# The first chunk of h and of the merged branches begins at the weights' place in a row of 256 bytes

## The chip, the core and the metric

The kernel runs on one core of one Trainium2 chip. The metric is the device time of one execution in microseconds (us); lower is better. TensorE (PE) multiplies matrices: it loads a stationary operand of 128 x 128 numbers (a weight load, shown as PEld) and then streams a moving operand past it. VectorE (DVE) and ScalarE (ACT) do elementwise work, GpSimd (POOL) little here, SyncE (SP) issues the DMAs that bring weights from memory into SBUF, the core's working memory of 128 partitions.

Addresses matter in this change. Every operand begins at some byte of its partition; this text calls that address modulo 256 the operand's **place**.

## The reference

Two layers on 256 tokens of width 2048, all in float32:

```python
h = rmsnorm(x, norm_mix[l]) * (1.0 + sc_a) + sh_a
qa, ka, va, qb, kb, vb, ga, gb = split_cols(h @ w_in[l])
ya = window_attention(...) @ w_proj_a[l]            # 8 heads of 128
yb = neighbourhood_attention(...) @ w_proj_b[l]     # 8 heads of 128
merged = sigmoid(ga) * ya + sigmoid(gb) * yb
x = x + gt_a * (merged @ w_out[l])
h = rmsnorm(x, norm_ffn[l]) * (1.0 + sc_m) + sh_m
u = depthwise_conv(h @ w_up[l], conv_w[l], conv_b[l])
g, v = split(u)                                     # 2 x 5632
x = x + gt_m * ((silu(g) * v) @ w_down[l])
```

The six modulation vectors (`sc_a`, `sh_a`, ...) are a matrix-vector product of `silu(c)` with `ada_w`.

## The kernel before

**Two-part numbers.** Each float32 factor is held as a high part and a rest, both in the type float32r. A product is three matmuls: high times high, high times rest, rest times high. `unit` brings 16 weight blocks of 128 x 128 in one DMA of 1 MB, then splits each half of them into `hl`: ACT copies the high part (L240), DVE subtracts (L241). There are 232 such units in a layer and four `hl` buffers, reused in turn.

**Two kinds of product.** `features` makes 128 output features for all 256 tokens: `feature_block` (L245 to L251) loads the weights (`hl`) as the stationary operand and streams the activation chunk as the moving one, 256 columns; L249 is weight-high with activation-high, L250 weight-high with activation-rest, L251 weight-rest with activation-high. These three lines, in this order, are one *group*; a block of outputs is one group per 128 rows of the contraction, 16 for `h` and `merged`. `tokens` (L325 to L327) makes q, k and v: there `h` is stationary and four weight blocks, 512 columns, are the moving operand.

**Order of the work.** In a layer: q, k, v and the first gate (in layer 0 the contraction is cut into parts of 2, 4, 5 and 5 chunks, in layer 1 it is whole), with attention heads interleaved in the background; the projection of branch A (`oA`, 8 chunks); the second gate from `h`; the projection of branch B (`oB`), merged and split into `merged`; `w_out` on `merged`; then the FFN in three rounds, each of up-projections from `h` and down-projections from the activations `act`. The modulation's weights are streamed past DVE (L172) at a written pace beside all this. The program's order is that of the code; every engine runs its own queue in that order and waits on semaphores.

**Places.** `OFF, ROW = 48, 64` are counted in 4-byte words: 192 and 256 bytes. The pools are laid out one after the other, and `skip` puts small unused tiles between them. The four `hl` buffers begin at place 32; in units that hold q, k or v weights the data starts `OFF` words later, at 224. `skip(4 * OFF)` (L120) moves the pool of `h` to place 224; `merged` takes the same tile in its turn. All chunks are multiples of 1024 bytes, so each of the 16 chunks of `h` and `merged` begins at 224, and so do the buffers of the pool `ev` behind it (tag `u`: the last two `oA`, some gates, the convolution's scratch), those of `at` (`p`, `pT`, `qn`) and, after `skip(64)`, the pool `s` with `oA`, `oB`, `act` and the packed q, k, v. So a feature group has its moving operand at 224 and its weights at 32, save where a unit of layer 0 holds both q/k/v blocks and gate blocks: there both are at 224. In `tokens` both operands are at 224.

Of the kernel before, what the change touches and what calls it, by code (L numbers as in the profile page):

```python
# [9 lines left out]
F32 = mybir.dt.float32  # L10
F32R = mybir.dt.float32r
# [4 lines left out]
P = 128  # L16
L = 2
D = 2048
S = 256
KC = D // P  # L20
# [77 lines left out]
OFF, ROW = 48, 64  # L98
# [7 lines left out]
def encoder(ctx: ExitStack, tc: tile.TileContext, a: dict, out: bass.AP):  # L106
# [4 lines left out]
    def skip(n, p=None):  # L111

        skips.append((p or pool(f"skip{len(skips)}", 1)).tile([P, n // 4], F32, name=f"skip{len(skips)}"))
        nc.vector.memset(skips[-1][:], 0.0)
# [2 lines left out]
    lay = pool("lay", 2)  # L117
    rawp = pool("raw", 4)
    hlp = pool("hl", 4)
    skip(4 * OFF)  # L120
    hp = pool("h", 1)
    ev = pool("ev", 3)
    at = pool("at", 2)
# [22 lines left out]
        nc.scalar.activation(out=cact[:, i : i + 512], in_=cb[:], func=AF.Silu)  # L146
    x = const.tile([P, KC, S], F32, name="x")
    skip(96, const)
    skip(64)
    sp = pool("s", 1)  # L150

    def place(tag, n, dt, name):
        return sp.tile([P, n, S], dt, name=name, tag=tag)

    def chunks_of(p, tag, n, name):

        t = p.tile([P, n, 2, S], F32R, name=name, tag=tag)
        return [t[:, k] for k in range(n)]

    mods, amods, nrms, done = {}, {}, {}, {0: 0, 1: 0}  # L160

# [170 lines left out]
    def split(dst, src):  # L332
        nc.scalar.copy(dst[:, 0], src)
        nc.vector.tensor_tensor(out=dst[:, 1], in0=src, in1=dst[:, 0].bitcast(F32), op=ALU.subtract)

    def warm(n):

        if n:
            ps = ax.tile([P, 512], F32, name="warm", tag="ax")
            for _ in range(n):  # L340
                tc.keep_in_program_order(nc.tensor.matmul(ps[:, :P], ident[:], ident[:], start=True, stop=True))
# [32 lines left out]

    def normed(l, w, sums, st, first=False):

        h = chunks_of(hp, "h", KC, f"h{l}_{w}")

        def steps():
            ss = mean_sq  # L380
            if not first:
                ss = sm.tile([P, 2], F32, name="nss", tag="nss")
                ins = nc.vector.tensor_tensor(out=ss[:], in0=sums.head[:], in1=sums.ps[:, 1], op=ALU.add)
                st.hold(ins.ins, HELD)
            rs = sm.tile([P, 2], F32, name="nrs", tag="nrs")
            nc.gpsimd.tensor_tensor(out=rs[:], in0=ss[:], in1=mhalf[:, :2], op=ALU.pow)
            if not first:
                warm(WARM[1])
            rb = ax.tile([P, 512], F32, name="rb", tag="ax")
            for t in range(2):  # L390
                tc.keep_in_program_order(
                    nc.tensor.transpose(rb[:, t * P : (t + 1) * P], rs[:, t : t + 1].broadcast_to([P, P]), ident[:])
                )
            warm(WARM_IN if first else WARM[2])
            if first:
                rbs = ev.tile([P, S], F32, name="rbs", tag="sqa", bufs=1)
                nc.scalar.copy(rbs[:], rb[:, :S])
                rb = rbs
            mod, amod = mods[l], amods[l]
            for kc in range(KC):  # L400
                if not first:
                    need(l, 48 * w + 2 * kc + 2)
                t = ev.tile([P, S], F32, name="ht", tag="z")
                sh = mod[:, 3 * w * KC + kc : 3 * w * KC + kc + 1]
                nc.vector.scalar_tensor_tensor(
                    out=t[:], in0=x[:, kc], scalar=amod[:, w, kc : kc + 1], in1=rb[:, :S], op0=ALU.mult, op1=ALU.mult
                )
                nc.scalar.activation(out=h[kc][:, 0], in_=t[:], func=AF.Identity, bias=sh)
                nc.vector.scalar_tensor_tensor(  # L409
                    out=h[kc][:, 1], in0=t[:], scalar=sh, in1=h[kc][:, 0].bitcast(F32), op0=ALU.add, op1=ALU.subtract  # L410
                )
                yield

        return h, steps()
# [89 lines left out]
    def urgent(yes):  # L504
        return tc.high_priority() if yes else nullcontext()
# [21 lines left out]
    def need(l, n):  # L527

        while done[l] < n:
            next(adas)  # L530
# [54 lines left out]
    for l in range(L):  # L585
        st = Stream(l) if l == 0 else nxt
        h, steps = normed(l, 0, None if l == 0 else sums, st, first=l == 0)
# [17 lines left out]
        def va(k, g):  # L605
            return packs[0][:, 2 * k + 1, g * HEAD : (g + 1) * HEAD]

        ready, heads = [0], [0]
        oA, oB = [], []

        def head_a(i):
            g = i // (HA // GA)
            if i >= 6:
                oA.append(ev.tile([P, 2, S], F32R, name=f"oA{l}_{i}", tag="u", bufs=2))
            elif i % 2 == 0:
                o = place(("y0", "y1", "y2")[i // 2], 4, F32R, f"oA{l}_{i}")
                oA.extend((o[:, :2], o[:, 2:]))
            yield
            yield from attend(
                qTa[:, i], kTa[:, g], lambda k: va(k, g), tables[0], SCALE, sink[:, i : i + 1], lambda: oA[i],  # L620
            )
# [105 lines left out]
        gb = []  # L727
        for tag in ("y0", "y1", "y2"):
            t = place(tag, 4, F32, f"gb{l}_{tag}")
            gb += [t[:, i] for i in range(4)]  # L730
        for i in range(2):
            t = ev.tile([P, 2, S], F32, name=f"gb{l}_{i}", tag="u", bufs=2)
            gb += [t[:, 0], t[:, 1]]

        def gate_b(mo):
# [5 lines left out]
        for mo in range(KC):  # L741
            st.features(hs, [gate_b(mo)])
        bg.finish(job)
        merged = chunks_of(hp, "h", KC, f"merged{l}")
        for mo in range(KC):

            def merge(ps):
# [29 lines left out]


        h, steps = normed(l, 1, sums, st)
        with urgent(True):  # L780
            for _ in range(FEED):
# [4 lines left out]
        def conv(ps, ch, u):  # L786
            w = cw[:, ch]
            nc.scalar.activation(out=u, in_=ps, func=AF.Identity, scale=w[:, 1:2], bias=w[:, 3:4])  # L788
            for j, to, of in ((0, slice(1, S), slice(0, S - 1)), (2, slice(0, S - 1), slice(1, S))):
                nc.vector.scalar_tensor_tensor(  # L790
                    out=u[:, to], in0=ps[:, of], scalar=w[:, j : j + 1], in1=u[:, to], op0=ALU.mult, op1=ALU.add
                )

        for gi, chunks in enumerate(FF_GROUPS):
            acts = []
            for tag, n in (("b0", 12), ("b1", 12), ("y1", 4), ("y2", 4)) if gi % 2 else (("o", 16), ("a", 12), ("y0", 4)):
                if len(acts) < len(chunks):
                    acts += chunks_of(sp, tag, n // 2, f"act{l}_{gi}_{tag}")
            acts = dict(zip(chunks, acts))
            sil = {}  # L800

            def g_evac(ps, c):
                u = sil[c] = ev.tile([P, 2, S], F32, name="u", tag="u", bufs=2)
                conv(ps, c, u[:, 0])
                nc.scalar.activation(out=u[:, 0], in_=u[:, 0], func=AF.Silu)

            def v_evac(ps, c):
                u = sil.pop(c)
                conv(ps, FC + c, u[:, 1])
                nc.vector.tensor_tensor(out=u[:, 1], in0=u[:, 1], in1=u[:, 0], op=ALU.mult)  # L810
                split(acts[c], u[:, 1])

            todo = list(chunks)
            if gi == 0:
                c0, c1 = todo[:2]
                todo = todo[2:]
                st.features(
                    hs, [lambda p: g_evac(p, c0), lambda p: v_evac(p, c0), lambda p: g_evac(p, c1), lambda p: v_evac(p, c1)]
                )
            for c in todo:  # L820
                st.features(hs, [lambda p: g_evac(p, c)])
                st.features(hs, [lambda p: v_evac(p, c)])
            if gi == len(FF_GROUPS) - 1:
                sums = Squares(f"ssf{l}") if l < L - 1 else None
            else:
                sums = None
            if gi == 0:
                need(l, 96)

            last = gi == len(FF_GROUPS) - 1  # L830

            def down(mo):
                def evac(ps):
                    residual(ps, mo, 5)
                    if last:
                        if l < L - 1:
                            sums.add(mo)
                        else:
                            nc.sync.dma_start(out[:, mo], x[:, mo])

                return evac

            for mos in OUT_TURNS:
                end = mos[0] == KC - 1
                ending = last and mos[0] >= ENDING
                if last and end and l < L - 1:
                    nxt = Stream(l + 1)
                    nxt.prefetch(AHEAD)
                with urgent(ending):
                    st.features([acts[c] for c in chunks], [down(mo) for mo in mos], sums.first if sums and end else None)  # L850
# [75 lines left out]
```

## Time and profile before

| what | value |
| --- | --- |
| time, median of 3 runs | 2740.95 us (2740.84 to 2763.34) |
| the profiled execution | 2756.37 us, of which its span is 2754.6 us |
| PE busy | 2697.4 us, 21,136 matmuls |
| PE weight loads busy | 2601.5 us |
| DVE / ACT busy | 2077.5 us (75%) / 1371.3 us (50%) |
| DMA | 700.36 MB, mean 254 GB/s |
| mean granted TensorE clock | 0.993 |

The profile tells of the one profiled execution. Busy times of PE are unions of overlapping records: matmuls are pipelined, one lasts about 280 ns in the records while the next starts some 115 ns after it. So what tells PE's rate is not the duration of a matmul but the distance between the starts of two, and this is read from the timeline or from the number of matmuls in a stretch of time. Starts are given to a hundredth of a microsecond.

### The profile page before, as it was taken

Reading aid. Unit: us, or ns where it says so; the run is one execution under the profiler, and the core shown is the slowest. Engines: PE = TensorE matmul, PEld = TensorE weight load, DVE = VectorE, ACT = ScalarE, POOL = GpSimd, SP = SyncE. Lnnn points to the kernel's source line nnn. Section 1 sums busy time; section 2 is a strip of 40 time slices with the busy share of each in tenths; the row PEclk is TensorE's granted clock in tenths of the full one; section 3 lists DMA queues with packets and bytes.
Section 4 is the critical chain, followed back from the end, with each engine's and each line's share of the span. In section 5 each row is a group of like instructions: output and inputs, shape, how many; then the busy total and the mean of one; then the engine's idle time right before and its main releaser. Section 6 shows DMA issues by size and latency. Waiting matters only on the chain.

```text
span 2754.6 us, 49972 instructions
## 1 busy us (share of the span) xinstructions
PE 2697.4 (98%) x21136; PEld 2601.5 (94%) x21136; DVE 2077.5 (75%) x2814; ACT 1371.3 (50%) x1897; POOL 39.3 (1%) x24
## 2 busy tenths in 40 slices
PE   7899999999999999999999999999999999999999
PEld 5788799998999999999988889999999999999999
DVE  6998987998887777678877665657888856665664
ACT  5344784444553455345444557544455535544553
POOL 0000100000000000000000000000000000000000
PEclk9999999999999999999999999999999999999999
DMA  8887588986778766677756556665858755555554
GB/s 317 334 333 262 219 303 326 349 337 242 275 283 316 277 248 252 253 277 284 280 197 258 220 211 247 234 249 203 294 221 301 264 192 191 199 192 191 199 188 149
DMA packets 101890, 700.36 MB, mean 254 GB/s; under 512 B 12705, under 2 KB 15009, under 8 KB 17697
## 3 DMA queue, kind: packets, MB, share of 16 engines
q1 hardware_dynamic: 101666, 697.17, 68.5%
q8 instruction: 165, 2.70, 0.4%
q14 instruction: 59, 0.48, 0.0%
HBM read 695.03 MB, written 2.10 MB: 253 GB/s over the span
## 4 chain that ended last, share of the span: by engine, by line
PE 73%; issue 15%; DVE 6%; DMA 2%; ACT 2%; POOL 1%; POOLq 0%; SPq 0%; ACTq 0%; DVEq 0%
PE ps L251 20%; PE ps L249 20%; PE ps L250 20%; PE ps_t L326 4%; PE ps_t L327 4%; PE ps_t L325 4%; DVE hl L241 2%; DVE aw L172 2%; DMA aw<-in_aw 1%; DMA w<-in_ws 1%; POOL qrs L373 1%; ACT hl L240 1%; PE sc L468 1%; PE po L499 1%; DVE qn L432 0%
## 5 line engine op out<-in xcount | busy, mean ns | idle before, releaser
L241 DVE TENSOR_TENSOR hl<-w,hl 128x1024 fp32r<-128x1024 f32 x928 | 1130.6, 1223 | 401.4 <-ACT hl L240 400.0
L240 ACT CAST hl<-w 128x1024 fp32r<-128x1024 f32 x928 | 971.1, 1049 | 850.8 <-PE ps L251 578.9
L249 PE MATMUL ps<-h,hl 128*128 128x256 f32 x3840 | 1073.8, 280 | 3.3 <-ACT hl L240 2.0
L251 PE MATMUL ps<-h,hl 128*128 128x256 f32 x3840 | 1073.6, 280 | 0.0
L250 PE MATMUL ps<-h,hl 128*128 128x256 f32 x3840 | 1072.7, 279 | 0.0
L250 PEld LDWEIGHTS ps<-h,hl 128*128 128x128 f32 x3840 | 728.8, 190 | 0.4
L249 PEld LDWEIGHTS ps<-h,hl 128*128 128x128 f32 x3840 | 723.9, 189 | 4.4 <-ACT hl L240 2.2
L251 PEld LDWEIGHTS ps<-h,hl 128*128 128x128 f32 x3840 | 722.9, 188 | 0.3 <-DVE hl L241 0.2
L172 DVE CUSTOM_DVE_ANT_0 aw<-aw,cact,ab 128x2048 f32<-128x2048 f32 x192 | 450.7, 2347 | 48.5 <-DMA aw<-in_aw 47.7
L790 DVE SCALAR_TENSOR_TENSOR u<-ps,cw,u 128x255 f32<-128x255 f32 x352 | 168.3, 482 | 104.0 <-ACT u L788 97.7
L325 PE MATMUL ps_t<-hl,h 128*128 128x512 f32 x576 | 227.9, 400 | 7.9 <-ACT hl L240 7.2
L326 PE MATMUL ps_t<-hl,h 128*128 128x512 f32 x576 | 228.5, 397 | 4.7 <-DVE hl L241 4.7
L327 PE MATMUL ps_t<-hl,h 128*128 128x512 f32 x576 | 227.5, 396 | 0.9 <-DVE h L409 0.9
L788 ACT ACTIVATE u<-ps,cw 128x256 f32<-128x256 f32 x176 | 98.7, 565 | 247.6 <-PE ps L251 247.6
L250 PE MATMUL ps<-merged,hl 128*128 128x256 f32 x512 | 144.3, 282 | 0.0
L249 PE MATMUL ps<-merged,hl 128*128 128x256 f32 x512 | 143.9, 282 | 0.3 <-DVE m L749 0.3
L251 PE MATMUL ps<-merged,hl 128*128 128x256 f32 x512 | 144.1, 281 | 0.0
L250 PE MATMUL ps<-act_o,hl 128*128 128x256 f32 x512 | 142.9, 279 | 0.0
L251 PE MATMUL ps<-act_o,hl 128*128 128x256 f32 x512 | 142.8, 279 | 0.0
L249 PE MATMUL ps<-act_o,hl 128*128 128x256 f32 x512 | 142.5, 279 | 0.0
L325 PEld LDWEIGHTS ps_t<-hl,h 128*128 128x128 f32 x576 | 109.6, 191 | 31.9 <-ACT hl L240 8.3
L326 PEld LDWEIGHTS ps_t<-hl,h 128*128 128x128 f32 x576 | 109.8, 191 | 30.4 <-DVE hl L241 8.1
(162 smaller groups left out, 3755.8 us busy)
## 6 DMA issues: line engine op xcount, KB each, us to landing
w<-in_ws SPq DMA_DIRECT2D x464, 1024.0 KB, 4.9
aw<-in_aw SPq DMA_DIRECT2D x192, 1024.0 KB, 5.0
bias<-in_bias SPq DMA_DIRECT2D x16, 256.0 KB, 5.1
x<-in_xT SPq DMA_DIRECT2D x4, 512.0 KB, 5.2
out<-x SPq DMA_DIRECT2D x16, 128.0 KB, 2.8
cw<-in_cw SPq DMA_DIRECT2D x2, 176.0 KB, 5.5
maskA<-in_maskA SPq DMA_DIRECT2D x1, 256.0 KB, 5.3
ab<-in_ab SPq DMA_DIRECT2D x2, 48.0 KB, 5.9
```

The lines of the kernel that those rows point to most:

```text
L172: nc.vector.tensor_tensor_reduce(out=raw[:], in0=raw[:], in1=cact[:], scale=1.0, scalar=ab[:, i : i + 1], op0=ALU.mult, op1=ALU.add, accum ...
L240: nc.scalar.copy(hl[:, 0], r)
L241: nc.vector.tensor_tensor(out=hl[:, 1], in0=r, in1=hl[:, 0].bitcast(F32), op=ALU.subtract)
L249: nc.tensor.matmul(out, hi, act[:, 0], start=first, stop=False)
L250: nc.tensor.matmul(out, hi, act[:, 1], start=False, stop=False)
L251: nc.tensor.matmul(out, lo, act[:, 0], start=False, stop=last)
L325: nc.tensor.matmul(ps[:], xh, hi, start=kc == kcs[0], stop=False)
L326: nc.tensor.matmul(ps[:], xh, lo, start=False, stop=False)
L327: nc.tensor.matmul(ps[:], xl, hi, start=False, stop=kc == kcs[-1])
L373: nc.gpsimd.tensor_tensor(out=dst, in0=src, in1=mhalf[:, :k], op=ALU.pow)
L788: nc.scalar.activation(out=u, in_=ps, func=AF.Identity, scale=w[:, 1:2], bias=w[:, 3:4])
L790: nc.vector.scalar_tensor_tensor(out=u[:, to], in0=ps[:, of], scalar=w[:, j : j + 1], in1=u[:, to], op0=ALU.mult, op1=ALU.add)
```

## The change

`chunks_of` for `h` and `merged` is replaced by `led`. The tile is 48 words longer and begins at place 32, since `skip(4 * OFF)` is gone; chunk 0 sits at its head (32), and chunks 1 to 15 follow after a hole of 192 bytes, at 224 as before. Together the pool takes as many bytes as before, so the buffers ahead of tag `u` stay where they were.

`paired` replaces the three allocations under tag `u`: each buffer is 64 bytes longer and its data starts 64 bytes in. The tag began at 224, so the first of the two buffers now has its data at 32, the second, 2112 bytes later, at 96. What lies behind it (`p`, `pT`, `qn` and others) moves by 128 bytes, to 96; `skip(192)` in place of `skip(64)` adds another 128, so that the pool `s` is at 224 again.

No instruction is added or reordered; one small memset of DVE at the start (the one of `skip(4 * OFF)`) goes.

```diff
-    skip(4 * OFF)
     hp = pool("h", 1)
...
-    skip(64)
+    skip(192)
     sp = pool("s", 1)
...
+    def led(name):
+
+        t = hp.tile([P, KC * 2 * S + OFF], F32R, name=name, tag="h")
+        at = [0] + [OFF + 2 * S * k for k in range(1, KC)]
+        return [t[:, i : i + 2 * S].rearrange("p (a s) -> p a s", a=2) for i in at]
+
+    def paired(dt, name):
+
+        t = ev.tile([P, 2 * S + ROW - OFF], dt, name=name, tag="u", bufs=2)
+        return t[:, ROW - OFF :].rearrange("p (a s) -> p a s", a=2)
...
-        h = chunks_of(hp, "h", KC, f"h{l}_{w}")
+        h = led(f"h{l}_{w}")
...
-                oA.append(ev.tile([P, 2, S], F32R, name=f"oA{l}_{i}", tag="u", bufs=2))
+                oA.append(paired(F32R, f"oA{l}_{i}"))
...
-            t = ev.tile([P, 2, S], F32, name=f"gb{l}_{i}", tag="u", bufs=2)
+            t = paired(F32, f"gb{l}_{i}")
...
-        merged = chunks_of(hp, "h", KC, f"merged{l}")
+        merged = led(f"merged{l}")
...
-                u = sil[c] = ev.tile([P, 2, S], F32, name="u", tag="u", bufs=2)
+                u = sil[c] = paired(F32, "u")
```

## The prediction

> **What bounds the kernel.** The page first:
>
> ```profile
> PE 2697.4 (98%) x21136; PEld 2601.5 (94%) x21136; DVE 2077.5 (75%) x2814; ACT 1371.3 (50%) x1897; POOL 39.3 (1%) x24
> ...
> PEclk9999999999999999999999999999999999999999
> ...
> PE 73%; issue 15%; DVE 6%; DMA 2%; ACT 2%; POOL 1%; POOLq 0%; SPq 0%; ACTq 0%; DVEq 0%
> ```
>
> PE is busy throughout and the chain that ends last is PE's, so time is the number of matmuls times their distance. The change adds no matmul; it can only change that distance. So the second view is the table of busy times by stretch, for PE alone, over the FFN of layer 0 and the FFN of layer 1, which run the same code:
>
> ```profile
> 690.00:1402.00 712.00, 712.00 (x6047) 1.00 0.74 273
> 2056.00:2742.00 686.00, 686.00 (x6055) 1.00 0.58 210
> ```
>
> The columns are stretch, length, PE busy (matmuls), granted clock, DMA share, GB/s. 712.00/6047 = 117.7 ns a matmul in layer 0, 686.00/6055 = 113.3 ns in layer 1, at the same granted clock of 1.00 and without a wait. PE thus runs at **two paces**: by the timeline a group of three (L249, L250, L251) takes 353.3 ns or 340.0 ns, without a mixture, for hundreds of us. The groups of instructions by line show the weight loads of part of the two stretches (700 to 1390 us, then 2060 to 2700 us):
>
> ```profile
> L250 PEld LDWEIGHTS ps<-h,hl 128*128 128x128 f32 x1311 | 252.0, 192 | 0.0
> L251 PEld LDWEIGHTS ps<-h,hl 128*128 128x128 f32 x1312 | 246.3, 188 | 0.0
> L249 PEld LDWEIGHTS ps<-h,hl 128*128 128x128 f32 x1311 | 246.2, 188 | 0.0
> ```
> ```profile
> L250 PEld LDWEIGHTS ps<-h,hl 128*128 128x128 f32 x1329 | 249.5, 188 | 0.0
> ```
>
> At the slow pace every third load takes 192 ns, at the quick one none does. (From 1800 to 2000 us, also slow, it is L249's: the third is fixed by the rhythm, not by the operand.) And a load runs beside the stream of the matmul before it. I read this as two steady rhythms between the stream of moving data and the load of the next weights, one with a collision in each three and one with none.
>
> There is a **third pace**, in this trace already: in layer 0's mixed units the weights lie at 224 like the moving operand. The timeline at the end of one of these:
>
> ```profile
> 132.11 0.28 PE L249 MATMUL ps<-h,hl 128*128 128x256 f32 x1
> 132.23 0.28 PE L250 MATMUL ps<-h,hl 128*128 128x256 f32 x1
> 132.35 0.28 PE L251 MATMUL ps<-h,hl 128*128 128x256 f32 x1
> 132.47 0.28 PE L249 MATMUL ps<-h,hl 128*128 128x256 f32 x1
> 132.59 0.28 PE L250 MATMUL ps<-h,hl 128*128 128x256 f32 x1
> 132.71 0.28 PE L251 MATMUL ps<-h,hl 128*128 128x256 f32 x1
> 132.83 0.28 PE L249 MATMUL ps<-h,hl 128*128 128x256 f32 x1
> 132.95 0.28 PE L250 MATMUL ps<-h,hl 128*128 128x256 f32 x1
> 133.07 0.28 PE L251 MATMUL ps<-h,hl 128*128 128x256 f32 x1
> 133.19 0.28 PE L249 MATMUL ps<-h,hl 128*128 128x256 f32 x1
> 133.30 0.28 PE L250 MATMUL ps<-h,hl 128*128 128x256 f32 x1
> 133.42 0.28 PE L251 MATMUL ps<-h,hl 128*128 128x256 f32 x1
> ```
>
> Up to 132.71 the starts are 0.12 apart: 360 ns a group. There the weights' place goes from 224 to 32, and from 132.83 to 133.19 a group takes 353: the slow pace from its first group, kept for 48 groups until the next mixed unit at 149.8. The loads of same-place stretches last 192 ns each (window 240 to 243 us, all three lines).
>
> ```profile
> L250 PEld LDWEIGHTS ps<-h,hl 128*128 128x128 f32 x9 | 1.7, 192 | 0.0
> ```
>
> Counting groups over the whole timeline: 6,272 in all, 2,932 quick, 3,202 slow, 44 at the same place, some 94 torn by waits or other matmuls. **What chooses the pace** is how a stretch began. After an interruption of PE either follows: slow from 563, 689, 1793 us, quick from 419, 1656, 2055 us. Where PE came without a gap from operands at the same place it was slow each time: at 132.83 and 216.53 from mixed units, at 327.69 and 1641.42 from q/k/v (both operands at 224). Four of four; no unbroken stretch went from same place to quick.
>
> **The change, part by part.**
>
> *Chunk 0 at 32.* Its groups have moving operand and weights at one place. There are 16 outputs a layer for the first gate (in layer 0 only the first part holds chunk 0), 16 for the second, 88 for up-projections, 16 for `w_out`: 136 a layer, 272 groups. Each should take 360: 6.7 ns more than slow, 20.0 more than quick. Against the slow pace 272 x 6.7 = 1.8 us.
>
> *What follows it.* This is the large term. With every output over 16 chunks PE leaves the same place anew without a gap, so a stretch no longer keeps the rhythm of its beginning. By the four transitions each such exit lands in the slow pace, and stays there over the down-projections and `oB`, which have no such chunk and follow without interruption. Then the 2,932 quick groups become slow: 2,932 x 13.3 = 39.1 us. The transitions of the trace moved the weights and left the moving operand at 224, here it is the other way round; I take them as equal since their difference is what both change.
>
> *`oA`.* Chunk 6 at 32 is again such a group (32 in all), chunk 7 at 96 a distance that no row shows: 96 matmuls. From below they go at the quick pace (-4.4 ns each against slow, -0.4 us), from above each load stands open: after a wait the second start came 0.22 us behind the first (562.57 to 562.79), 102 ns over the slow pace, 9.8 us. I take the same-place distance, 120 ns, nearest in kind: 0.2 us, and as much again for chunk 6. Of the quick groups counted, some 170 belong to `oA`, where attention interrupts PE; half may stay quick: -1.1 us.
>
> *Tokens.* Chunk 0 of `h` as the weights at 32 beside a stream at 224: 54 matmuls a layer, 108. Their distance is 227 ns for 512 columns, twice 113.3: nothing to gain by this reading, or 6.7 ns each, 0.7 us. In layer 0's mixed units 24 matmuls have weights at 224 and chunk 0 at 32, unknown likewise: at 102 ns at most 2.4 us, taken as nothing.
>
> *Attention.* `p`, `pT` and `qn` go to 96: L456, L493 and L499 have 360 records; at 6.7 ns either way 2.4 us, taken as nothing, between waits that hide it.
>
> *DVE and ACT* read and write the same shapes (L790 482 ns, L788 565 ns) at other places. From 700 to 1390 us DVE is busy 545 of 690 us and ACT 327, so a tenth more still hides behind PE; in a stretch without that cover each us would count. The dropped memset is one of three of 72 to 98 ns, at 0.8 us, before the data it would wait for: nothing.
>
> Sum: 39.1 + 1.8 + 0.4 - 1.1 = +40.2 us on the execution's own 2756.4 (span 2754.6 and 1.8 around it): **2796.6 us**. The median shown, 2740.95, is 15.4 us below this execution, as much as 1,160 groups at 13.3 ns; the three runs lie 22.5 apart. Such distances are what stretches beginning in one rhythm or the other give, so I take no profiling cost off: where all is slow there is nothing left to vary. That is 2.0% over the median.
>
> **Rivals.**
>
> 1. *The exit lands in the quick pace.* For it: quick is as steady as slow, the four transitions moved the other operand, and at 59.33 us, after a same-place unit and a gap of 41 ns, quick came. Then 3,202 x 13.3 = 42.7 us go and 272 x 20.0 = 5.4 come: 2756.4 - 37.3 = 2719.1, 0.8% under the median. It decides from the first exit: if the group after chunk 0 takes 340, this one wins. Against it: four of four.
>
> 2. *The place isn't what sets the pace*, or a passage through one group leaves the rhythm as it was. The Trainium skill, page "SBUF — State Buffer", section "SBUF: two separate sides", holds that on the engines' side only the port pair of VectorE and GpSimd contends and that PE never waits on anyone; by that rule places do not matter and the time stays. Against this stand the rows: 120.0 ns at the same place, 117.8 or 113.3 apart, in one stage, at one clock. In this case either nothing changes or chunk 0 costs 272 x 6.7 to 20.0 = 1.8 to 5.4 us; by the runs shown 2741 to 2768.
>
> 3. *The change doesn't do what it says*, in that 96 instead of 32 for the second buffer decides: the 9.8 us above, added to any of the others.
>
> **How the numbers follow.** The forecast gets 0.60, rival 1 0.26, rival 2 0.14, and rival 3 is inside their bounds. The forecast's own range is 2785 (a quarter of the quick groups survive) to 2803 (part of the unknown distances). To hold 8 in 10 the range must take in rival 1: 2714 to 2803. More than 1% from the median, about what a measurement of this kernel can tell, begins at 2713.5 and 2768.4. Rival 1 passes the lower only if the transitions are cheap or the kernel before runs slower than its median: 0.10 of its 0.26. The rest of it and rival 2 are within 1%, save 0.01 each way: faster 0.11, same 0.28, slower 0.61.
>
> **What would show it.** In the timeline of the FFN of layer 1 a group of 360 ns at each chunk 0 and then 353 ns, where 340 stood; matmuls of L250 from `h` at 281 ns in both layers; 6,055 matmuls in 713 us instead of 686; and `act` at the same pace as `h`. A group of 340 after chunk 0 makes the forecast wrong, as does an FFN that keeps one pace right through chunk 0.

## The result, and the profile after

The changed kernel takes 2730.01 us (median of 18 runs, 2726.04 to 2735.50); the kernel before took 2742.24 in 18 runs beside it (2729.41 to 2774.38). The ratio on record, which leaves out runs more than 1.5% above their kernel's fastest, is 0.994, with a 95% interval of 0.9917 to 0.9963: a gain of 0.6%, where 2.0% of loss was forecast. The two medians above differ by 0.45%. The spread shrank too, from 45 us to 9.5. In a later group of runs the kernel before lay at 2756.16 in 33 runs (2727.30 to 2788.69) and the changed one at 2729.73 in 11 (2727.03 to 2735.28). So the changed kernel runs about where the kernel before ran at its best, and runs there every time.

The page of the changed kernel (its lines are numbered ten higher than before: L259, L260, L261 are the group, L251 the split on DVE):

```profile
PE 2669.1 (98%) x21136; PEld 2572.8 (94%) x21136; DVE 2073.0 (76%) x2813; ACT 1371.0 (50%) x1897; POOL 39.3 (1%) x24
...
PEclk9899999999999999999999999999999999999999
...
PE 70%; issue 16%; DVE 6%; DMA 5%; ACT 1%; POOL 1%; POOLq 0%; SPq 0%; ACTq 0%; DVEq 0%
```

PE is still what bounds it: 28.3 us less busy (2697.4 before), and the span is 27.4 us shorter. The table by stretch, for PE alone, over unbroken parts of both FFNs (stretch, length, PE busy and matmuls, granted clock, DMA share, GB/s):

```profile
931.00:1381.00 450.00, 450.00 (x3964) 1.00 0.74 273
2031.00:2720.00 689.00, 689.00 (x6067) 1.00 0.59 208
```

That is 113.5 and 113.6 ns a matmul in *both* layers, where it was 117.7 in layer 0 and 113.3 in layer 1. The weight loads of the first of these stretches, by line:

```profile
L260 PEld LDWEIGHTS ps<-h,hl 128*128 128x128 f32 x877 | 164.7, 188 | 0.0
L259 PEld LDWEIGHTS ps<-h,hl 128*128 128x128 f32 x877 | 164.7, 188 | 0.0
L261 PEld LDWEIGHTS ps<-h,hl 128*128 128x128 f32 x877 | 164.7, 188 | 0.0
```

No line has the 192 ns loads of the slow pace any more. What happens at a chunk 0 is seen in the timeline; the start at 692.62 is chunk 0, at the place 32, and 692.98 is chunk 1, at 224 again:

```profile
692.26 0.28 PE L259 MATMUL ps<-h,hl 128*128 128x256 f32 x1
692.38 0.28 PE L260 MATMUL ps<-h,hl 128*128 128x256 f32 x1
692.50 0.28 PE L261 MATMUL ps<-h,hl 128*128 128x256 f32 x1
692.62 0.28 PE L259 MATMUL ps<-h,hl 128*128 128x256 f32 x1
692.74 0.28 PE L260 MATMUL ps<-h,hl 128*128 128x256 f32 x1
692.86 0.28 PE L261 MATMUL ps<-h,hl 128*128 128x256 f32 x1
692.98 0.29 PE L259 MATMUL ps<-h,hl 128*128 128x256 f32 x1
693.10 0.28 PE L260 MATMUL ps<-h,hl 128*128 128x256 f32 x1
693.22 0.28 PE L261 MATMUL ps<-h,hl 128*128 128x256 f32 x1
693.34 0.28 PE L259 MATMUL ps<-h,hl 128*128 128x256 f32 x1
693.46 0.28 PE L260 MATMUL ps<-h,hl 128*128 128x256 f32 x1
693.57 0.28 PE L261 MATMUL ps<-h,hl 128*128 128x256 f32 x1
693.68 0.28 PE L259 MATMUL ps<-h,hl 128*128 128x256 f32 x1
```

A wait has left PE slow here (0.36 us from 692.26 to 692.62). It goes through chunk 0, still slow, and comes out quick: 0.34 us from 693.34 to 693.68. Counted over the whole timeline, in outputs of 16 chunks that no wait interrupts and whose three lines come in order: 216 of 216 passages through chunk 0 of `h` or `merged` that began quick ended quick, and 7 of 7 that began slow ended quick.

One output in each layer has its lines in another order, the last but one of `w_out`. There the program issues the first product of the next output ahead of its turn (that output then begins with L260, at 645.64), so that *four* matmuls in a row, not three, have their moving operand at 32:

```profile
639.39 0.28 PE L259 MATMUL ps<-merged,hl 128*128 128x256 f32 x1
...
639.73 0.39 PE L259 MATMUL ps<-merged,hl 128*128 128x256 f32 x2
639.96 0.28 PE L260 MATMUL ps<-merged,hl 128*128 128x256 f32 x1
640.08 0.28 PE L261 MATMUL ps<-merged,hl 128*128 128x256 f32 x1
640.20 0.28 PE L259 MATMUL ps<-merged,hl 128*128 128x256 f32 x1
...
640.55 0.28 PE L259 MATMUL ps<-merged,hl 128*128 128x256 f32 x1
```

This passage began quick (340 ns a group up to 639.73) and ended slow: from the third group on a group takes 353 ns, to the end of the output. The same output of layer 1 did the same. So what is said below of a step of the moving operand holds for three matmuls, one chunk, and not for any number of them.

The sum goes as follows, in time over 340 ns a group. Before: 3,202 slow groups, 43.6 us in all groups that no wait tears. After: 745 slow groups, 9.6 us, and 13.1 us in all. That is 30.5 us less. Some 210 of the 745 are not at the slow pace: they are the group behind a chunk 0, at 351 ns, in a passage from quick to quick. Torn groups cost 5.5 us more (26.9 to 32.4); L259's wait for the split on ACT grew from 2.0 to 4.0 us. That a quicker PE runs into more waits does not explain it: by a like count the changed kernel has 31.5 us and 31.7 in its second profile, but two kernels below that are as quick, both without `paired`, have 27.4 and 27.8, and the kernel before 26.2. What causes it is open. The remaining 2.4 us of the 27.4 lie outside these groups; the first product of features began that much earlier (54.09 us, 56.45 before), and no run tells whether the change did that.

### The profile page after: what moved, and what is told of

The parts are those of the page before. It is cut to its first block, busy times and chain, and to the rows that moved or that the text cites. A ratio compares the mean times of both kernels' runs of the same rounds, so it can differ in the third digit from the quotient of the medians.

```text
span 2727.2 us, 49971 instructions
## 1 busy us (share of the span) xinstructions
PE 2669.1 (98%) x21136; PEld 2572.8 (94%) x21136; DVE 2073.0 (76%) x2813; ACT 1371.0 (50%) x1897; POOL 39.3 (1%) x24
## 4 chain that ended last, share of the span: by engine, by line
PE 70%; issue 16%; DVE 6%; DMA 5%; ACT 1%; POOL 1%; POOLq 0%; SPq 0%; ACTq 0%; DVEq 0%
PE ps L259 18%; PE ps L261 18%; PE ps L260 18%; DMA aw<-in_aw 4%; PE ps_t L336 4%; PE ps_t L337 4%; PE ps_t L335 4%; DVE hl L251 2%; DVE aw L182 2%; DMA w<-in_ws 1%; ACT hl L250 1%; POOL qrs L383 1%; PE po L509 1%; PE sc L478 1%; PE tp L503 0%
## 5 line engine op out<-in xcount | busy, mean ns | idle before, releaser
L251 DVE TENSOR_TENSOR hl<-w,hl 128x1024 fp32r<-128x1024 f32 x928 | 1129.7, 1222 | 369.1 <-ACT hl L250 368.3
L259 PE MATMUL ps<-h,hl 128*128 128x256 f32 x3840 | 1069.0, 279 | 4.0 <-ACT hl L250 4.0
L261 PE MATMUL ps<-h,hl 128*128 128x256 f32 x3840 | 1067.1, 278 | 0.0
L260 PE MATMUL ps<-h,hl 128*128 128x256 f32 x3840 | 1065.7, 278 | 0.0
L259 PEld LDWEIGHTS ps<-h,hl 128*128 128x128 f32 x3840 | 723.6, 189 | 5.2 <-ACT hl L250 4.4
L260 PEld LDWEIGHTS ps<-h,hl 128*128 128x128 f32 x3840 | 723.9, 189 | 0.5
L261 PEld LDWEIGHTS ps<-h,hl 128*128 128x128 f32 x3840 | 723.8, 188 | 0.3
L259 PE MATMUL ps<-merged,hl 128*128 128x256 f32 x512 | 141.9, 278 | 0.7 <-DVE m L759 0.7
L261 PE MATMUL ps<-act_o,hl 128*128 128x256 f32 x512 | 142.1, 278 | 0.3 <-DVE hl L251 0.3
L261 PE MATMUL ps<-merged,hl 128*128 128x256 f32 x512 | 142.1, 278 | 0.0
L260 PE MATMUL ps<-merged,hl 128*128 128x256 f32 x512 | 142.1, 277 | 0.0
L260 PE MATMUL ps<-act_o,hl 128*128 128x256 f32 x512 | 142.0, 277 | 0.0
L259 PE MATMUL ps<-act_o,hl 128*128 128x256 f32 x512 | 141.6, 277 | 0.0
L336 PEld LDWEIGHTS ps_t<-hl,h 128*128 128x128 f32 x576 | 109.6, 190 | 30.5 <-DVE hl L251 8.0
```

Source lines behind the costliest of these rows:

```text
L251: nc.vector.tensor_tensor(out=hl[:, 1], in0=r, in1=hl[:, 0].bitcast(F32), op=ALU.subtract)
L259: nc.tensor.matmul(out, hi, act[:, 0], start=first, stop=False)
L260: nc.tensor.matmul(out, hi, act[:, 1], start=False, stop=False)
L261: nc.tensor.matmul(out, lo, act[:, 0], start=False, stop=last)
L336: nc.tensor.matmul(ps[:], xh, lo, start=False, stop=False)
```

## The experiments

**How the rival causes are told apart.** In the kernel before, four transitions had led from the same place to the slow pace; in the changed kernel the passage leads to the quick pace. Two things differ. In the trace of before it was the *weights* whose place stepped while the moving operand stayed at 224; in the change it is the *moving operand*. And those stays at the same place were long, while chunk 0 is three matmuls. Theory A holds that the operand that steps decides, theory B that the length does. Where no number of runs is given, a kernel ran once, and the kernel before took 2763 to 2788 us beside it: there the paces in the trace decide, not the time.

### A long stay at the same place

```diff
-        at = [0] + [OFF + 2 * S * k for k in range(1, KC)]
+        at = [2 * S * k + (OFF if k > 3 else 0) for k in range(KC)]
```

> Chunks 0 to 3 of h and of merged at 32 instead of chunk 0 alone; all else as in the changed kernel. Theory A (the step of the moving operand from one place to another resets the rhythm, and the reset lands in the quick pace): the twelve same-place matmuls take about 120 ns each, the step out of them lands quick again, groups of 340 ns over chunks 5 to 15; about 20 ns more for each of three further chunks, 272 x 60 ns = 16 us over the changed kernel's 2729, some 2745 us. Theory B (a same-place passage of three matmuls is too short to settle, a long one settles at 120 ns and its exit is slow, as at 132.83 and 216.53 us of the kernel before): groups of 353 ns over chunks 4 to 15, about 2800 us.

Measured: 2740.17 us. The timeline around the step out; chunk 3 begins at 804.00, chunk 4 at 804.36:

```profile
804.00 0.28 PE L259 MATMUL ps<-h,hl 128*128 128x256 f32 x1
804.12 0.28 PE L260 MATMUL ps<-h,hl 128*128 128x256 f32 x1
804.24 0.28 PE L261 MATMUL ps<-h,hl 128*128 128x256 f32 x1
804.36 0.29 PE L259 MATMUL ps<-h,hl 128*128 128x256 f32 x1
804.48 0.28 PE L260 MATMUL ps<-h,hl 128*128 128x256 f32 x1
804.60 0.28 PE L261 MATMUL ps<-h,hl 128*128 128x256 f32 x1
804.72 0.28 PE L259 MATMUL ps<-h,hl 128*128 128x256 f32 x1
804.83 0.28 PE L260 MATMUL ps<-h,hl 128*128 128x256 f32 x1
804.95 0.28 PE L261 MATMUL ps<-h,hl 128*128 128x256 f32 x1
805.06 0.28 PE L259 MATMUL ps<-h,hl 128*128 128x256 f32 x1
```

Chunk 3 runs at the settled 360 ns, and two groups later it is 340. All 226 undisturbed passages of four chunks end quick, each costing 80 ns against the quick pace instead of 20. A longer stay does not lead to the slow pace: theory B falls. Length still matters in a way that neither theory has: four matmuls at 32 led to the slow pace above, three and twelve lead to the quick one, and so did the thirteen of this run's two outputs in the other order.

### Another place than the weights'

```diff
-        at = [0] + [OFF + 2 * S * k for k in range(1, KC)]
+        at = [32] + [OFF + 2 * S * k for k in range(1, KC)]
```

> Chunk 0 of h and of merged at 160 instead of 32, all else as in the changed kernel. Theory A (any step of the moving operand's place resets the rhythm): quick groups of 340 ns after each chunk 0, 2725 to 2735 us; only the cost of the three matmuls of chunk 0 differs. Rival (the weights' own place is what does it): the FFN keeps the rhythm in which a stretch began, or goes slow: 2740 to 2800 us.

Measured: 2732.54 us; 225 of 225 undisturbed passages of three matmuls from quick end quick, at 53 ns each instead of 20; the two of four matmuls end slow here too. The same place is not needed. A step of the moving operand to 160 does as well and costs more.

### The weights step instead

The kernel before, with the first weight block of an up-projection laid at 224:

```diff
+            if j == 0 and blocks[0][0] == "w_up" and len({mo for _, _, mo in blocks}) == 1:
+                first = hl[:, OFF : OFF + 2 * P].rearrange("p (a n) -> p a n", a=2)
+                rest = hl[:, 5 * ROW : 5 * ROW + 2 * (n - P)].rearrange("p (a n) -> p a n", a=2)
+                for part, src in ((first, r[:, :P]), (rest, r[:, P:])):
+                    nc.scalar.copy(part[:, 0], src)
+                    nc.vector.tensor_tensor(out=part[:, 1], in0=src, in1=part[:, 0].bitcast(F32), op=ALU.subtract)
+                halves.append((first, rest))
+                continue
```

> The kernel before, with its moving operands all at 224; in the units of the up-projections that hold one output, the first weight block lies at 224 too, the other fifteen at 32, so that three matmuls of each such output run at the same place, reached by a step of the weights and not of the moving operand. Theory A (the moving operand's step is what resets to quick; a step of the weights lands slow, as at 132.83 and 216.53 us of the kernel before): both FFNs slow at 353 ns a group, 2780 to 2800 us. Theory B (it is the shortness of the same-place passage, whichever operand moves): both FFNs quick at 340 ns a group but for the first two groups of an output, 2725 to 2740 us.

Measured: 2788.66 us. The split of one block on its own adds 168 instructions to ACT and 168 to DVE, off the path. By stretch, layer 1 before the first step, then both FFNs behind it:

```profile
2036.00:2052.00 16.00, 16.00 (x144) 1.00 0.40 137
...
840.00:1400.00 560.00, 560.00 (x4754) 1.00 0.73 271
2090.00:2740.00 650.00, 650.00 (x5516) 1.00 0.56 203
```

The FFN of layer 1 begins quick: its first four outputs are interleaved and have no weight step, and 57 groups of 340 ns were counted there. With the steps both FFNs run at 117.8 ns, down-projections included. All 166 undisturbed passages end slow, the two that began quick too. The same distance, reached for the same three matmuls, gives the other pace when the other operand steps.

### The same place throughout, and other distances

```diff
-    skip(4 * OFF)
...
-        at = OFF if streamed else 0
+        at = 0
```

> The kernel before with every moving operand of a product of features at 32, the weights' place, and with both operands of tokens at 32 as well: the same place throughout. All theories: 360 ns a group everywhere, 2932 x 20.0 + 3202 x 6.7 = 80 us over the kernel before's profiled 2756, some 2836 us, and no difference from run to run in the pace. If a place equal to the weights' were harmless in itself, it would stay near 2740 us.

Measured: 2830.35 us. By stretch, layers 0 and 1:

```profile
710.00:1410.00 700.00, 700.00 (x5836) 1.00 0.73 271
2100.00:2800.00 700.00, 700.00 (x5836) 1.00 0.56 202
```

119.9 ns a matmul in both, as the same-place stretches of before promised, and all three lines' loads take 192 ns. Two more, with `OFF` at 32 and at 16 words and nothing stepping:

> The kernel before with OFF at 32 words: all moving operands of features at 160, 128 bytes from the weights at 32, and tokens with both operands at 160; no operand steps. Theory A says nothing of which paces this distance has. Two ways: the two rhythms of the kernel before are a matter of its distance of 64 bytes and others have other paces, between 340 and 360 ns a group; or every distance but zero has the same two, and the time is one of the kernel before's, 2727 to 2789 us.

> The same with OFF at 16 words: moving operands at 96, tokens with both at 96. The same two ways as for 160.

```diff
-OFF, ROW = 48, 64
+OFF, ROW = 32, 64
```

At 160 it took 2821.71 us: the FFN of layer 0 ran at 118.6 ns a matmul (5,901 in 700 us), that of layer 1 at 119.9. At 96 it took 2789.43 us, both FFNs at 353.3 ns a group throughout, and without the 192 ns loads. So a distance has its own paces, and of the four tried the 64 bytes from 224 to 32 is the only one whose FFN was seen at 340 ns. At 96, 226 groups of the first gates and of `oA` did run at 340 ns, so this distance has the quick pace too; that its FFN can't have it is not shown.

### Both operands step together

The moving operand's chunk 0 at 160 and, by the edit of the weights above, the first weight block at 224, so that their distance stays 64 bytes:

```diff
-        at = [0] + [OFF + 2 * S * k for k in range(1, KC)]
+        at = [32] + [OFF + 2 * S * k for k in range(1, KC)]
```

> Without paired; chunk 0 of h and merged at 160, and in the units of the up-projections that hold one output the first weight block at 224, so that there both operands step together and their distance stays the 64 bytes that it has at 224 and 32. If only the distance between the two operands counts (theory A1), the passage leaves the rhythm as it was, and each FFN keeps one pace, quick or slow, through chunk 0: 2727 to 2789 us, groups of one output like those before it. If the moving operand's step acts by itself (theory A2), every up-projection is quick after chunk 0: 2725 to 2740. If the weights' step acts by itself and comes last (theory A3), every one is slow: 2780 to 2800.

Measured: 2761.83 us, and none of the three had it right. In the up-projections the outputs *alternate*: 83 of 83 passages that begin quick end slow, 83 of 83 that begin slow end quick. So the pace after a passage can depend on the one before. The two passages of four matmuls in `w_out`, where only the moving operand steps, went from quick to slow here as well: nine of nine in the five profiles that have such passages undisturbed.

### Parts of the change, and two variants

Without `paired` (tag `u` at 224 as before, `skip(64)`); then chunk 2 in place of chunk 0; then a stepping chunk in the down-projections too:

```diff
-        t = ev.tile([P, 2 * S + ROW - OFF], dt, name=name, tag="u", bufs=2)
+        t = ev.tile([P, 2 * S], dt, name=name, tag="u", bufs=2)
...
+        at = [OFF + 2 * S * k for k in range(KC)]
+        at = [at[1], at[2], 0] + at[3:]
...
+            t = sp.tile([P, 2 * S + ROW - OFF], F32R, name=f"kick{l}_{gi}", tag="kick")
+            acts[1] = t[:, ROW - OFF :].rearrange("p (a s) -> p a s", a=2)
```

> The changed kernel again, as the yardstick of this group: about 2730 us, and most of it at 340 ns a group by the theory of the moving operand's step (theory A).

> The changed kernel without paired: the buffers under tag u and all behind them are at 224 again, only chunk 0 of h and of merged steps to 32. If the gain is all in the step of h and merged, 2730 us as the changed kernel, within 3 us; if the steps of oA 6 and 7 (32 and 96) bring part of it, some 170 groups of the stages around oA would lose up to 13.3 ns each, 2.3 us; if they only cost, 64 groups of about 20 ns, up to 1.3 us less.

> As led_only, but chunk 2 of h and merged sits at 32 instead of chunk 0. Theory A: which chunk steps does not matter in a long unbroken stretch; after an interruption, which comes at the start of an output, the reset comes two chunks into it and not a whole output later. The changed kernel has some 100 slow groups of this kind in the first gate of layer 1 and some 50 in the second part of layer 0: 2 us off, some 2728. If the first chunk matters as such (the start of a new accumulation), the FFN keeps one pace or goes slow: 2740 to 2800.

> As chunk2, and in each round of the FFN the second activation chunk sits in a tile of its own at 32, so that the down-projections step too. Theory A: 96 more passages at 20 ns cost 1.9 us; what they bring is the slow groups that a wait leaves in down-projections, 141 in the changed kernel's profile, 1.9 us: 2725 to 2730, and a smaller spread between runs.

| kernel, 11 runs each on one chip | median us | lowest to highest | slow groups in its profile |
| --- | --- | --- | --- |
| the changed kernel | 2729.73 | 2727.03 to 2735.28 | 640 |
| without `paired` | 2729.33 | 2724.91 to 2732.01 | 922 |
| and chunk 2 instead of 0 | 2727.12 | 2724.68 to 2734.10 | 475 |
| and a step in down-projections | 2733.44 | 2727.15 to 2738.83 | 552 |

The gain is the step of `h` and `merged`; `paired` adds nothing that can be measured. Chunk 2 does what chunk 0 does, so a chunk need not be the first. In the output of `w_out` whose lines come in another order, the fourth matmul is then not at 32, and it stays quick in both layers. Its 2.6 us against the changed kernel are the size that was expected, but not told apart from nothing: resampling both sets of 11 gives a ratio of 0.9990, from 0.9978 to 1.0004. The steps in the down-projections missed their expectation, 2725 to 2730 us and a smaller spread: the median is 6.3 us over that of the kernel with chunk 2 alone (resampled ratio 1.0023, from 1.0006 to 1.0032), and the spread grew from 9.4 to 11.7 us. Their 20 ns a passage are seen, 1.9 us for 96 of them, and the slow groups that they were to remove were few by then; where the rest comes from is not shown. The last column counts the group behind each passage too, over 200 in each kernel.

### Both steps in one output, apart from each other

Weights step at chunk 0, moving operand at chunk 8:

```diff
+        at = [OFF + 2 * S * (k + (k < 8)) if k != 8 else 0 for k in range(KC)]
```

> Without paired; chunk 8 of h and merged at 32, the other chunks at 224, and in the units of the up-projections that hold one output the first weight block at 224, so that in each such output the weights step at chunk 0 and the moving operand steps at chunk 8. Theory A (a step of the weights lands slow, a step of the moving operand lands quick, from either pace): every such output has some seven slow groups of 353 ns after chunk 0 and seven quick ones of 340 ns after chunk 8; 168 outputs x 7 x 13.3 ns = 15.7 us, and 168 x 20 ns = 3.4 us for the weights' passages, over led_only's 2729, some 2748 us. If the pace after a passage depended on the pace before it, as where both operands step together, the outputs would differ among themselves: 2730 to 2765.

Measured: 2780.88 us, and the expectation fell: 166 of the 168 passages at chunk 8 of these outputs began slow and ended slow. (The other two stand in the first single output of each FFN, which follows a wait of over 3 us and starts at 640 ns a group; there the weight step had left no slow pace.) But not in the same slow pace. It has three phases, told by which of the three loads takes 192 ns. After chunk 0 it is the first line's, after chunk 8 the third's, and the next weight step brings the first back. With this, the passages of three matmuls in which one operand steps, the moving one to 32 or the weights to 224, fell into one table in the traces of all runs:

| passage | quick | slow, 1st load long | slow, 2nd | slow, 3rd |
| --- | --- | --- | --- | --- |
| moving operand to 32 and back, three matmuls | quick | **slow, 3rd** | quick | quick |
| weights to 224 and back, three matmuls | slow, 1st | slow, 1st | not seen | slow, 1st |

Behind the entries stand, in outputs of 16 chunks without a wait: from slow with the first load long 167 passages here (166 in up-projections, one in a gate) and one each without `paired` and with chunk 2; with the second long three; with the third long 6 in the changed kernel's first profile, 6 in its second and 8 without `paired`. A single step of the moving operand is then not always enough, but two are, as long as no weight step comes between: without `paired`, at 1778 us, a passage left the slow pace slow and the next ended it. To 160 it may differ: the one passage there that met the first load long, at 1918 us, ended quick. The table was fitted after the fact, so it was tried on a pattern that nothing else foretells: weights at chunk 0, moving operand at chunks 5 and 10.

```diff
+        at = [OFF + 2 * S * (k + (k < 5) + (k < 10)) for k in range(KC)]
+        at[5], at[10] = 0, 2 * S
```

> As two_steps (the weights step at chunk 0 of an up-projection), but chunks 5 and 10 of h and merged at 32, so that the moving operand steps twice in an output. Theory C (the slow pace has three phases, told by which of the three loads takes 192 ns; a passage of the moving operand leads from quick to quick, from slow with the second or the third load long to quick, from slow with the first load long to slow with the third long; a passage of the weights leads from any of them to slow with the first load long): in every such output slow groups with the first load long after chunk 0, slow with the third long after chunk 5, quick after chunk 10, and quick down-projections behind the last; against two_steps' 2781 some 168 x 5 x 13.3 = 11 us and some 1,200 groups of down-projections, 16 us, less: about 2754 us. Rival D (where the weights step in an output, no step of the moving operand can reach the quick pace): all slow as in two_steps, 2775 to 2790.

Measured: 2755.12 us. The weight loads in one output (L271, L272, L273 are the group here), in three windows: behind chunk 0 (939.5 to 940.7 us), behind chunk 5 (941.6 to 942.4) and behind chunk 10 (943.6 to 944.5):

```profile
L271 PEld LDWEIGHTS ps<-h,hl 128*128 128x128 f32 x4 | 0.8, 192 | 0.0
L272 PEld LDWEIGHTS ps<-h,hl 128*128 128x128 f32 x4 | 0.8, 188 | 0.0
L273 PEld LDWEIGHTS ps<-h,hl 128*128 128x128 f32 x4 | 0.8, 188 | 0.0
```
```profile
L271 PEld LDWEIGHTS ps<-h,hl 128*128 128x128 f32 x3 | 0.6, 188 | 0.0
L272 PEld LDWEIGHTS ps<-h,hl 128*128 128x128 f32 x3 | 0.6, 188 | 0.0
L273 PEld LDWEIGHTS ps<-h,hl 128*128 128x128 f32 x2 | 0.4, 192 | 0.0
```
```profile
L273 PEld LDWEIGHTS ps<-h,hl 128*128 128x128 f32 x4 | 0.8, 188 | 0.0
L272 PEld LDWEIGHTS ps<-h,hl 128*128 128x128 f32 x3 | 0.6, 188 | 0.0
L271 PEld LDWEIGHTS ps<-h,hl 128*128 128x128 f32 x3 | 0.6, 188 | 0.0
```

First line long, third line long, none. The passage at chunk 5 met the first load long in 166 of the 168 outputs, the one at chunk 10 met the third load long in the same 166 and ended quick in all 168, and the down-projections behind them ran at 340 ns. The other two are again the first single output of each FFN, behind its wait.

## Why the prediction was wrong, step by step

- **PE's distance between starts is all that counts, and it has three paces**: right. The same place throughout gives the third pace everywhere; its time had been worked out at some 2836 us and was 2830.35.
- **Chunk 0's group takes 360 ns**: too high. The pace needs time to settle. From quick, the three matmuls start 119, 113 and 117 ns apart (349 ns in the passage at 801.84 us), and the group behind takes 351; with four chunks it was settled in the fourth. A passage costs 20 ns over the quick pace, spread over two groups, which by accident is the 20.0 that the rival's sum had for one.
- **Every exit lands slow**: this step failed, and with it the forecast. The working said that the transitions of the trace moved the weights, the change the moving operand, and "I take them as equal since their difference is what both change". All four transitions were weight steps, those from q/k/v too, for there the moving operand was at 224 before and after. Weight steps do land slow: the run with a weight step had 166 of 166. A step of the moving operand over three matmuls lands quick; over four, which the working did not foresee either, it lands slow. So the 39.1 us had the wrong sign; in its place slow groups fell from 3,202 to 745.
- **The pace carries over into stages without such a chunk**: right, with the other pace: both FFNs' unbroken stretches, down-projections among them, are quick.
- **`oA`, tokens, attention, ACT and DVE**: the terms were small, and leaving `paired` out changed the median by 0.4 us. In `oA` the two stepping chunks in a row do not lead out of the slow pace: 7 of 7 such passages that began slow ended slow, and 13 of 13 that began quick ended quick.
- **The median shown differs from the profiled execution by the pace in which stretches happen to begin**: borne out. The kernel before ranged from 2727 to 2789 us; the changed one, where passages settle it, from 2726 to 2736.
- **Rival 1** named the mechanism, 2719.1 us, with 0.26. Against this sum the profiled execution, 2729.0 us, has 9.9 us more. Untorn groups hold 13.1 us where the sum leaves 6.3 (5.4 for passages and 0.9 for the 44 groups at the same place): 6.8 us, for it had no group slow. Torn groups add 5.5, and 2.4 go off outside. The groups that stayed slow are some 140 in layer 0's second to fourth parts, which hold no chunk 0; 141 in down-projections after waits; 28 behind the passages of four matmuls; most others in the first output after an interruption by attention, until the next chunk 0, and in `oA`.
- **Rival 2**, that places do not matter or that a passage leaves the pace as it was: the runs disagree. All moving operands at 32 instead of 224, with tokens' operands following, took 2830 us against 2727 to 2789 for the kernel before, at a granted clock of 1.00 in the FFNs of both, and passages through one chunk changed the pace in both directions. The rule of the Trainium skill's page "SBUF — State Buffer", section "SBUF: two separate sides", that PE never waits on anyone, was read as if places could not matter. The runs contradict this reading; whether PE's own two operands stand in each other's way in SBUF, they do not show.

The forecast's evidence was four cases that all shared one condition, which the change did not.

## What to carry to other kernels

Where every matmul loads new weights, the start addresses of the moving and the stationary operand modulo 256 bytes can set PE's rate: here 340, 353 or 360 ns for the same three matmuls. If one program has two paces for the same code, count the starts in unbroken stretches before explaining a run-to-run spread otherwise, and look for something that puts the pace back at regular points; one chunk whose moving operand begins elsewhere did this for 20 ns a time. Check in the timeline how many matmuls that step really holds: here a fourth, let in by the order of the program, turned its effect around. And when a trace offers a few transitions as evidence, ask which operand moved in them.

## What was not expected of the hardware

The two paces at the distance of 64 bytes are steady: 2,021 groups in a row at 353.3 ns, 2,020 at 340.0, with the pace kept until a wait or a step. The slow pace has a period of three matmuls, with one load in three at 192 ns instead of 188, and three phases that react differently to the same step. Moving operand and weights are not alike: a step of one over three matmuls leads to the quick pace, of the other to the slow one, of both at once from each to the other; and a step of the moving operand over four matmuls leads to the slow one. Why, no run here shows. The settling takes several matmuls, so it is not a matter of the one matmul at another place, and whether it lies in the reading of SBUF or in the handing over of weights stays open.
